# A down projection that runs one Winograd product at a time over all features, with act's operand sums stored by the up projection

## The chip, the cores and the metric

One Trainium2 chip, one core. The metric is the device time of one execution in microseconds (us). The kernel computes a whole decoder layer in one launch; the change lies in its last part, the feed-forward network.

## What is computed

The reference is one hybrid decoder layer over 2048 tokens of 1024 features in float32. The part that matters here is its feed-forward network:

```
def conv_gated_ffn(h, w_up, conv_w, conv_b, w_down):      # h: 2048 x 1024, w_up: 1024 x 8192, w_down: 4096 x 1024
    u = h @ w_up
    u_pad = jnp.pad(u, ((0, 0), (CONV_WIDTH - 1, 0), (0, 0)))
    u = conv_b + sum(conv_w[j] * u_pad[:, j:j + S] for j in range(CONV_WIDTH))
    gate, val = jnp.split(u, 2, axis=-1)
    return (jax.nn.gelu(gate, approximate=True) * val) @ w_down
...
        f = conv_gated_ffn(rms_norm(x, norm_ffn_pre[l]), w_ffn_up[l], conv_w[l], conv_b[l], w_ffn_down[l])
        x = x + rms_norm(f, norm_ffn_post[l])
```

## The kernel before

Phases a and b (normalisation, input projections, attention, the recurrent branch, the output projection) fill the first 1,215 us and are not touched. `phase_d` is the feed-forward network: the up projection, the convolution and the gate make `act` (4096 features by 2048 tokens), which goes to DRAM; the down projection reads it back and makes the output.

**Products in parts.** An operand is split into a high part (a cast on ScalarE, L40) and a low part (a subtraction on VectorE, L41), and a product of two blocks is three products of parts (`mm3`, L25 to L31). Every matmul of `phase_d` has a 128 x 128 stationary and a 128 x 512 moving operand.

**Up projection.** The work is 64 pairs n (32 pairs of a gate and a value block of 128 columns, for each half of 1,024 tokens). A pair is a 2 x 2 x 2 block product in Winograd's seven products j = 0 to 6, each 12 matmuls. `slots` is the order of the products; the pairs of two neighbours are interleaved, so that one product of another pair lies between two of one pair. `wprep` makes the weights' part `LEAD` = 6 products ahead. Each product has its own bank, and the eight banks go round; `post` combines them on VectorE: seven additions that read a bank for each pair (L284), and one copy on ScalarE (L289). Then the convolution (L275 to L277), GELU and the product with the value half follow, and 128 features by 1,024 tokens of `act` are stored (L308).

**Down projection.** Again Winograd's seven products, on blocks of 512 tokens (A) and 512 columns (B), for two halves h of the tokens and four groups g of 1,024 features: 56 steps (h, g, p) in the order `ORD` = P1, P5, P7, P6, P2, P3, P4 within each (h, g). A step is 4 blocks of 128 tokens, 12 matmuls each, 48 in all. `dload` loads a quarter of an operand (1 MB), `dprep` splits two of them (128 x 2048 each) one step ahead, and `dsums` makes Winograd's operand sums from the raw quarters, on GpSimd and VectorE (L191). Each block of a step goes into a bank and from there is copied (g = 0, L412) or added on VectorE (L414) to an accumulator in SBUF, one for each product. After the last group, `merge` (L395) adds the accumulators up, `square` (L378, L379) takes the sums of squares and scales by column, and `finish` (L386 to L391) norms, adds the residual and stores.

**Order.** The kernel's text gives dependencies and a priority; the framework orders each engine's instructions, and the DMA issues of each queue, when it builds the program. On the chip every queue then runs in that order. All DMAs of the part run on SyncE's queue, but for three at the start of the down projection.

Of the kernel before, what the change touches and what calls it, by code (L numbers as in the profile page):

```python
# [24 lines left out]
def mm3(nc, out, terms, first=True, last=True):  # L25
    """out += sum over terms of lhsT.T @ rhs, each operand an exact (hi, lo) pair"""
# [17 lines left out]
def rstd(nc, pool, ss, scale, eps, mhalf, tag):  # L44
    """(ss * scale + eps) ** -0.5"""
# [8 lines left out]
def bias_lines(nc, pool, psum, rel_bias, onehot, neg, line_d):  # L54
    """the bias of each relative position, masked, as 128 equal rows per head"""
# [12 lines left out]
def hsum(nc, pool, tag, h2t, hq, k):  # L68
    """Winograd's combinations of the blocks of h2 (features by tokens), for feature tiles k and k + 4"""
# [10 lines left out]
def conv_consts(nc, cw, pt, conv_w, conv_b, rows, ident):  # L80
    """the taps and the bias of the convolution, features on partitions: columns (tap, block)"""
# [8 lines left out]
LEAD = 6  # L90
# [3 lines left out]
def phase_d(ctx, tc, x1, h2t, w_up, cw, halo, w_down, g_post, mhalf, out, hq, act):  # L94
# [6 lines left out]
    with ExitStack() as es:  # L101
        rp = es.enter_context(tc.tile_pool(name="dr", bufs=2))
        # fourteen places of 8 KB
# [13 lines left out]
        def bank():  # L117
            """the eight banks in turn"""
            pss.append(pss.pop(0))
            return pss[-1].tile([P, 512], F32, tag="b", name="b")  # L120

        G = 8
        NG = NU // G
        NH = SEQ // SB
        ORD = ("P1", "P5", "P7", "P6", "P2", "P3", "P4")
        # operands of each product, in the places of the blocks that their sums replace
        OPS = {"P1": ("A11", "B11"), "P5": ("A21", "B11"), "P7": ("A11", "B12"), "P6": ("A11", "B11"),
               "P2": ("A12", "B21"), "P3": ("A12", "B22"), "P4": ("A22", "B21")}
        # sums made once a product is split: place, minuend, other, operation
        AFTER = {"P1": (("B11", "B12", "B11"), ("A11", "A11", "A21"), ("A21", "A22", "A21+"), ("B12", "B22", "B12")),  # L130
                 "P7": (("B11", "B22", "B11"), ("A11", "A22", "A11")),
                 "P2": (("A12", "A12", "A11"), ("B21", "B21", "B11"))}
        FREE = {"P5": ("A21",), "P7": ("B12",), "P2": ("A11", "B11"), "P3": ("A12", "B22"), "P4": ("A22", "B21")}
        wdv = w_down.rearrange("(j c p) d -> j p c d", p=P, c=G // 2)
# [3 lines left out]
        ACC = ({"P1": 10, "P5": 12, "P7": 2, "P6": 3, "P2": 13, "P3": 11}, {"P1": 10, "P5": 2, "P7": 3, "P6": 13, "P2": 11, "P3": 12})  # L138
        PARTS = ((4, 5, 6, 7), (0, 1, 8, 9))
        XT = {"A21": 8, "B12": 10, "A11": 12, "B11": 14}  # L140
        raw, dops, acc, pools, phases = {}, {}, {}, {}, []
        for h in range(NH):
            for g in range(NG):
                phases += [(h, g, p) for p in ORD]

        def dload(h, g, x, q=None):
# [6 lines left out]
            elif (h, g, x) == (0, 0, "B12"):  # L153
                t = big(ACC[0]["P3"], x, F32)
            else:
                t = pools["raw"].tile([P, 4, 512], F32, name=x)
# [1060 lines left out]
```

## Time and profile before

| | before |
|---|---|
| median of 3 runs (lowest to highest) | 3253.43 us (3253.23 to 3253.59) |
| span of the profiled execution, first to last instruction | 3251.4 us |
| TensorE busy | 3085.7 us, 95% of the span |
| VectorE busy | 2657.5 us, 82% |
| ScalarE busy | 1439.1 us, 44% |
| GpSimd busy | 1219.2 us, 37% |
| moved by DMA | 388.25 MB |

The profiled execution has no time of its own beside its span; the median of the runs is 2.0 us above that span, so the two agree to 0.1%. PE is TensorE's matmuls, PEld its weight loads, DVE VectorE, ACT ScalarE, POOL GpSimd, SP SyncE's queue. Matmuls are pipelined, so the durations of single matmuls overlap; the pace is read from how many fit into a stretch.

### The profile page before, as it was taken

How to read it: one execution, taken by the hardware profiler on the slowest of the kernel's cores; microseconds unless marked ns; L12 is line 12 of the kernel's file. 1: busy time of each engine (PE TensorE's matmuls, PEld its weight loads, DVE VectorE, ACT ScalarE, POOL GpSimd, SP SyncE). 2: the span in 40 equal slices, each digit the busy share in tenths (PEclk: the TensorE clock that was granted, in tenths of full speed). 3: DMA queues.
4: the chain of work that ended last, by engine and by line, in shares of the span. 5: the costliest groups of instructions: out<-in, count | busy, mean ns of one | idle time of the engine just before them, and what ended most of it. 6: DMA issues, size and time to landing. Idle time of an engine off the chain costs nothing. (4 is left out here: it accounts for less than half of the span.)

```text
span 3251.4 us, 46480 instructions
## 1 busy us (share of the span) xinstructions
PE 3085.7 (95%) x17897; PEld 2463.4 (76%) x17897; DVE 2657.5 (82%) x3535; ACT 1439.1 (44%) x2277; POOL 1219.2 (37%) x857
## 2 busy tenths in 40 slices
PE   5999999989999998899999999999999999889996
PEld 3888888777777777788888877888887777667775
DVE  4779786766767768999999999999998688886887
ACT  4565646354444454334444444444443533244322
POOL 1203122123334434533433433334333443784347
PEclk8999999979999999999999999999999999989998
DMA  5546463654445536422222342222223423142232
GB/s 134 143 137 180 131 169 105 186 170 119 133 120 174 180 122 206 144 84 85 85 78 78 97 150 78 79 90 85 78 78 105 154 104 104 65 155 104 104 104 78
DMA packets 476458, 388.25 MB, mean 119 GB/s; under 512 B 114042, under 2 KB 401100, under 8 KB 475212
## 3 DMA queue, kind: packets, MB, share of 16 engines
q1 hardware_dynamic: 474652, 382.13, 37.6%
q8 instruction: 141, 2.31, 0.3%
q10 hardware_dynamic: 1584, 3.15, 0.3%
q14 instruction: 81, 0.66, 0.1%
HBM read 276.68 MB, written 108.53 MB: 118 GB/s over the span
## 5 line engine op out<-in xcount | busy, mean ns | idle before, releaser
L30 PE MATMUL b<-hh,wh 128*128 128x512 f32 x1792 | 709.3, 396 | 18.5 <-DVE uv L284 12.8
L30 PE MATMUL b<-do 128*128 128x512 f32 x2688 | 651.4, 405 | 70.8 <-DVE do L41 54.7
L30 PE MATMUL b<-hl,wh 128*128 128x512 f32 x1792 | 710.2, 396 | 2.0 <-DVE hl L41 2.0
L30 PE MATMUL b<-hh,wl 128*128 128x512 f32 x1792 | 709.4, 396 | 0.4 <-DVE wl L41 0.4
L30 PEld LDWEIGHTS b<-do 128*128 128x128 f32 x2688 | 521.3, 195 | 200.7 <-DVE do L41 63.6
L40 ACT CAST wh<-wr 128x512 fp32r<-128x512 f32 (+1 forms) x400 | 279.8, 705 | 469.8 <-DMA wr<-in_w_ffn_up 152.7
L41 DVE TENSOR_TENSOR wl<-wr,wh 128x512 fp32r<-128x512 f32 (+1 forms) x400 | 368.6, 923 | 75.2 <-ACT wh L40 74.1
L30 PEld LDWEIGHTS b<-hh,wh 128*128 128x128 f32 x1792 | 338.2, 189 | 102.6 <-ACT wh L40 9.4
L30 PEld LDWEIGHTS b<-hl,wh 128*128 128x128 f32 x1792 | 338.3, 189 | 83.5 <-DVE hl L41 3.3
L30 PEld LDWEIGHTS b<-hh,wl 128*128 128x128 f32 x1792 | 338.3, 189 | 80.4 <-DVE wl L41 1.3
L237 POOL TENSOR_TENSOR s<-wr 128x512 f32<-128x512 f32 x64 | 133.6, 2087 | 610.2 <-DMA wr<-in_w_ffn_up 598.5
L30 PE MATMUL pj<-hh,wh 128*128 128x512 f32 x640 | 256.8, 402 | 27.8 <-ACT t L574 25.1
L30 PE MATMUL pj<-hh,wl 128*128 128x512 f32 x640 | 254.4, 398 | 0.1
L30 PE MATMUL pj<-hl,wh 128*128 128x512 f32 x640 | 254.1, 398 | 0.0
L41 DVE TENSOR_TENSOR do<-hr,do 128x2048 fp32r<-128x2048 f32 x48 | 151.1, 3151 | 47.2 <-ACT do L40 47.1
L40 ACT CAST do<-hr 128x2048 fp32r<-128x2048 f32 x48 | 90.5, 1905 | 212.9 <-PE b L30 131.3
L246 POOL TENSOR_TENSOR wr<-wr,s 128x512 f32<-128x512 f32 x64 | 140.4, 2193 | 110.8 <-DVE wl L41 110.7
L30 PEld LDWEIGHTS pj<-hh,wh 128*128 128x128 f32 x640 | 122.1, 191 | 56.1 <-ACT t L574 26.8
L414 DVE TENSOR_TENSOR acc<-acc,b 128x512 f32<-128x512 f32 x168 | 110.4, 679 | 44.8 <-PE b L30 44.8
L30 PEld LDWEIGHTS pj<-hh,wl 128*128 128x128 f32 x640 | 122.2, 191 | 27.2 <-DVE wl L41 0.9
L30 PEld LDWEIGHTS pj<-hl,wh 128*128 128x128 f32 x640 | 122.2, 191 | 25.9 <-DVE hl L41 0.2
L275 ACT ACTIVATE yg<-ug,cw 128x1024 f32<-128x1024 f32 x64 | 79.7, 1246 | 139.3 <-DVE ug L284 139.3
(290 smaller groups left out, 5847.8 us busy)
## 6 DMA issues: line engine op xcount, KB each, us to landing
wr<-in_w_ffn_up SPq DMA_DIRECT2D x128, 512.0 KB
wr<-in_w_in SPq DMA_DIRECT2D x64, 512.0 KB
d_act<-yg SPq DMA_DIRECT2D x64, 512.0 KB
B<-in_w_ffn_down SPq DMA_DIRECT2D x22, 1024.0 KB
wr<-d_act SPq DMA_DIRECT2D x16, 1024.0 KB
xt<-in_x SPq DMA_DIRECT2D x28, 512.0 KB
d_bk<-bk SPq DMA_DIRECT2D x16, 512.0 KB
wr<-in_w_in SPq DMA_DIRECT2D x32, 256.0 KB
```

The source lines that it names most:

```text
L30: nc.tensor.matmul(out=out, lhsT=a, rhs=b, start=first and i == 0 and j == 0, stop=last and i == n - 1 and j == 2)
L40: nc.scalar.copy(out=hi, in_=raw)
L41: nc.vector.tensor_tensor(out=lo, in0=raw, in1=hi, op=ALU.subtract)
L237: tt(out=r[1], in0=t[:, 2], in1=t[:, 3], op=ALU.add)
L246: tt(out=t[:, 1], in0=t[:, 1], in1=r[2], op=ALU.subtract)
L275: nc.scalar.activation(out=y, in_=u[:, 2:], func=AF.Identity, scale=w2c[:, col:col + 1], bias=bc[:, col:col + 1])
L414: nc.vector.tensor_tensor(out=o, in0=o, in1=pd, op=ALU.add)
```

## The change

**Up projection.** Products that are only added now add up in a bank: products 0, 2, 5 and 6 of a pair run into one bank (three banks take turns), product 1 into another, 3 and 4 into another (five take turns). Between two products of a bank its state is read: ScalarE copies it after products 0, 2, 3 and 6, VectorE adds it to something after 1, 4 and 5. That is three additions and four copies a pair, where there were seven and one. `LEAD` is 5 and there are 6 buffers of weight parts instead of 7. The second pair's products 1 to 6 no longer stand beside those of the first pair at the start.

**act.** Once two feature blocks are done, the seven operands that the down projection takes from them are stored, the four sums among them made on VectorE (2) and GpSimd (2): 1.75 MB for two pairs, where it was 1 MB.

**Down projection.** 56 steps (p, k): for each product p in the order P5, P3, P2, P1, P6, P7, P4 all eight groups k of 256 features (of each half of the features), for both halves of the tokens: 8 blocks of 6 matmuls in 8 banks. A bank is emptied only at the last k of a product, and P3, P6, P7 and P4 go on adding to what the product before them left in it. The sums of results that `merge` made are so made in the banks; P5, P3 and P2 end in a copy to SBUF, P1, P6 and P7 in an addition to it, P4 in the final norm straight from the bank. Each step loads its operand of act (1 MB) and one or two quarters of w_down's blocks (0.5 MB each); GpSimd makes the weights' sum for P5, P6, P7 and P4, and those of P5 and P6 are stored in DRAM (`td`) for P6 and P4.

The diff, cut to the lines that are added in `phase_d` (those that they replace are in the functions printed above):

```diff
...
+LEAD = 5
+WB = 6
...
+def phase_d(ctx, tc, x1, h2t, w_up, cw, halo, w_down, g_post, mhalf, out, hq, act, td):
...
         def places(st, ids, side):
...
         def big(i, name, dtype=F32R):
...
+        def bank(i):
+            return pss[i].tile([P, 512], F32, tag="b", name="b")
...
+        KC = 8
+        ORD = ("P5", "P3", "P2", "P1", "P6", "P7", "P4")
+        AIDX = {"P5": 0, "P6": 1, "P7": 2, "P3": 3, "P1": 4, "P2": 5, "P4": 6}
+        CHAIN = ("P3", "P6", "P7", "P4")
+        wdv = w_down.rearrange("(m c p) (d n) -> c d p m n", p=P, c=2, d=2)
...
+        phases = [(p, k) for p in ORD for k in range(KC)]
+        raw, dops = {}, {}
+        OPL = ((0, 1, 4), (5, 6, 7))
+        def dload(i):
...
+            p, k = phases[i]
+            ar = rp.tile([P, 2, 2, 512], F32, tag="hr", name="ar")
+            for h in range(NH):
+                nc.sync.dma_start(out=ar[:, h], in_=act[h][k][AIDX[p]].rearrange("m p t -> p m t"))
+            br = rp.tile([P, 2, 2, 512], F32, tag="wr", name="br")
+            w = lambda c, d: wdv[c, d, :, 2 * k:2 * k + 2, :]
+            t = lambda j: td[k][j].rearrange("m p n -> p m n")
+            src = {"P5": (w(0, 1), w(0, 0)), "P3": (w(1, 1),), "P2": (w(1, 0),), "P1": (w(0, 0),), "P6": (w(1, 1), t(0)),
+                   "P7": (w(1, 1), w(0, 1)), "P4": (w(1, 0), t(1))}[p]
+            for j, a in enumerate(src):
+                nc.sync.dma_start(out=br[:, j], in_=a)
+            if len(src) == 2:
+                nc.gpsimd.tensor_tensor(out=br[:, 0], in0=br[:, 0], in1=br[:, 1], op=ALU.subtract)
+            if p in ("P5", "P6"):
+                nc.sync.dma_start(out=t(p == "P6"), in_=br[:, 0])
+            raw[i] = ar, br
+        def dprep(i):
+            if i >= len(phases):
+                return
+            ar, br = raw.pop(i)
+            ah, al, b = (big(j, "do") for j in OPL[i % 2])
+            split(nc, b[:, 0:2], b[:, 2:4], br[:, 0])
+            split(nc, ah, al, ar.rearrange("p h k t -> p (h k) t"))
+            dops[i] = ah, al, b
...
+            wp = us.enter_context(tc.tile_pool(name="dw", bufs=WB))
...
             def hprep(half, j):
...
             def wprep(n, j):
...
+            banks, sums, us_, ys, even = {}, {}, {}, {}, {}
+            turn = [0]
             def product(n, j):
...
+                if j == 0:
+                    banks[n, "a"] = bank(n % 3)
+                elif j in (1, 3):
+                    banks[n, "b"] = bank(3 + turn[0] % 5)
+                    turn[0] += 1
+                o = banks[n, "b" if j in (1, 3, 4) else "a"]
+                for k in range(4):
+                    for i, (a, b) in enumerate(((wh, hh), (wh, hl), (wl, hh))):
+                        nc.tensor.matmul(out=o, lhsT=a[:, k, :], rhs=b[:, k, :], start=j in (0, 1, 3) and k == 0 and i == 0,
+                                         stop=k == 3 and i == 2, skip_group_check=True)
             def utile(n, b):
...
+                y = tp.tile([P, SB], F32, name="yg" if b == 0 else "yv", bufs=3 - 2 * b)
...
             def post(n, j):
...
+                a, b = banks.get((n, "a")), banks.get((n, "b"))
+                def add(out, x, y):
+                    nc.vector.tensor_tensor(out=out, in0=x, in1=y, op=ALU.add)
+                if j in (0, 2, 3):
+                    sums[n, j] = ep.tile([P, 512], F32, name="sum", bufs=3)
+                    nc.scalar.copy(out=sums[n, j], in_=b if j == 3 else a)
                 elif j == 1:
...
+                    add(utile(n, 0)[:, 2:514], sums.pop((n, 0)), b)
                 elif j == 4:
...
+                    add(us_[n, 0][:, 514:], sums.pop((n, 2)), b)
...
                 elif j == 5:
...
+                    add(utile(n, 1)[:, 514:], sums.pop((n, 3)), a)
...
+                    nc.scalar.copy(out=us_[n, 1][:, 2:514], in_=a)
...
+                    k, m = ff // 4, ff // 2 % 2
+                    dst = act[half][k][:, m].rearrange("j p t -> p j t")
+                    if ff % 2 == 0:
+                        nc.sync.dma_start(out=dst[:, 4], in_=y[:, :512])
+                        even[0] = y
+                        return
+                    nc.sync.dma_start(out=dst[:, 5:7], in_=y.rearrange("p (j t) -> p j t", j=2))
+                    e = even.pop(0)
+                    s = rp.tile([P, 4, 512], F32, tag="hr", name="sa")
+                    V, Q = nc.vector.tensor_tensor, nc.gpsimd.tensor_tensor
+                    Q(out=s[:, 2], in0=e[:, :512], in1=e[:, 512:], op=ALU.subtract)
+                    V(out=s[:, 0], in0=e[:, 512:], in1=y[:, 512:], op=ALU.add)
+                    V(out=s[:, 1], in0=s[:, 0], in1=e[:, :512], op=ALU.subtract)
+                    Q(out=s[:, 3], in0=y[:, :512], in1=s[:, 1], op=ALU.subtract)
+                    nc.sync.dma_start(out=dst[:, 0:4], in_=s)
...
+            pos = {14 * (n // 2) + 2 * j + n % 2 * 7: (n, j) for n in range(N) for j in range(7)}
+            pos[1] = pos.pop(7)
+            slots = [pos[k] for k in sorted(pos)]
...
                 if n == N - 1:
...
+                        dload(0)
+                    elif j == 3:
...
+                        dload(1)
...
+            xts, acc = {}, {}
+            APL = {"C22": (2, 3), "C12": (8, 9), "C11": (10, 11)}
+            def xload(t):
+                xts[t] = fp.tile([P, D], F32, name="xt", bufs=3)
+                nc.sync.dma_start(out=xts[t], in_=x1v[t])
+            def square(t, i, o):
+                junk = ep.tile([P, 512], F32, tag="sum", name="junk", bufs=3)
...
+            def scale(d, o):
+                nc.gpsimd.tensor_tensor(out=o, in0=o, in1=gpost[:, d * 512:d * 512 + 512], op=ALU.mult)
             def finish(t, parts):
...
+                    if o.space == PSUM:
+                        r = ep.tile([P, 512], F32, tag="sum", name="r", bufs=3)
+                        nc.vector.scalar_tensor_tensor(out=r, in0=o, scalar=rs, in1=gpost[:, ds], op0=ALU.mult, op1=ALU.mult)
+                        nc.vector.tensor_tensor(out=r, in0=r, in1=xt[:, ds], op=ALU.add)
+                        o = r
+                    else:
+                        nc.vector.scalar_tensor_tensor(out=o, in0=o, scalar=rs, in1=xt[:, ds], op0=ALU.mult, op1=ALU.add)
...
+            bks = {}
+            for i, (p, k) in enumerate(phases):
+                dprep(i + 1)
+                dload(i + 2)
+                ah, al, b = dops.pop(i)
+                last = k == KC - 1
+                if last and p in ("P6", "P4"):
+                    for q in range(3):
+                        xload(4 * (p == "P4") + q)
+                for h in range(NH):
+                    for q in range(4):
+                        n = h * 4 + q
+                        if k == 0 and p not in CHAIN:
+                            bks[n] = bank(n)
+                        for m in range(2):
+                            a = slice(q * P, q * P + P)
+                            for j, (x, y) in enumerate(((ah, m), (ah, 2 + m), (al, m))):
+                                nc.tensor.matmul(out=bks[n], lhsT=x[:, 2 * h + m, a], rhs=b[:, y], start=k == 0 and p not in CHAIN and m == 0 and j == 0,
+                                                 stop=last and m == 1 and j == 2, skip_group_check=True)
+                        if not last:
+                            continue
+                        t = h * 8 + q + 4 * (p in ("P7", "P4"))
+                        name = {"P5": "C22", "P3": "C12", "P2": "C11", "P1": "C11", "P6": "C12", "P7": "C22", "P4": "C21"}[p]
...
+                            square(t, 0, bks[n])
+                            finish(t, [bks[n], acc["C22", h][:, q]])
+                        else:
+                            if q == 0 and p in ("P5", "P3", "P2"):
+                                acc[name, h] = big(APL[name][h], "acc", F32)
+                            o = acc[name, h][:, q]
+                            if p in ("P5", "P3", "P2"):
+                                nc.scalar.copy(out=o, in_=bks[n])
+                            else:
+                                nc.vector.tensor_tensor(out=o, in0=o, in1=bks[n], op=ALU.add)
+                                square(t, p != "P1", o)
+                                scale(p != "P1", o)
+                            if p == "P6":
+                                finish(t, [acc["C11", h][:, q], o])
+                        if p in ("P6", "P4") and n < 5:
+                            xload((n + 3) // 4 * 8 + (n + 3) % 4 + 4 * (p == "P4"))
...
```

Outside `phase_d` only the DRAM tiles differ:

```diff
-    act = [dp.tile([8, P, SEQ], F32, name=f"d_act{j}") for j in range(4)]
+    act = [[dp.tile([7, 2, P, 512], F32, name=f"d_act{h}_{k}") for k in range(8)] for h in range(2)]
+    td = [dp.tile([2, 2, P, 512], F32, name=f"d_td{k}") for k in range(8)]
```

## Rows read from the trace of the kernel before

**Rows 1.** The page: busy us of each engine; 40 equal slices of the span, in tenths.

```profile
PE 3085.7 (95%) x17897; PEld 2463.4 (76%) x17897; DVE 2657.5 (82%) x3535; ACT 1439.1 (44%) x2277; POOL 1219.2 (37%) x857
...
PE   5999999989999998899999999999999999889996
...
PEclk8999999979999999999999999999999999989998
```

**Rows 2.** Windows: busy us (instructions) of PE, PEld, DVE, ACT, POOL; clock; DMA share; GB/s.

```profile
0.00:1215.00 1215.00, 1160.28 (x9753) 917.27 (x9755) 863.08 (x1754) 631.69 (x1307) 320.70 (x457) 0.97 0.51 147
1215.00:2511.00 1296.00, 1273.75 (x5464) 1024.86 (x5461) 1200.42 (x1424) 548.53 (x738) 508.04 (x281) 0.99 0.30 99
2511.00:3234.00 723.00, 651.62 (x2690) 521.29 (x2688) 580.47 (x339) 257.48 (x229) 381.17 (x108) 0.95 0.31 107
3234.00:3252.00 18.00, 0.00 (x0) 0.00 (x0) 13.55 (x21) 1.45 (x4) 9.32 (x14) 0.60 0.61 233
```

**Rows 3.** The same windows, a stretch inside the up projection.

```profile
1460.00:1622.00 162.00, 162.00 (x698) 130.96 (x697) 151.17 (x191) 66.16 (x93) 60.19 (x33) 1.00 0.27 85
```

**Rows 4.** Groups of PE, 1215 to 2511: busy, mean ns; idle before, releasers.

```profile
L30 PE MATMUL b<-hh,wh 128*128 128x512 f32 x1792 | 709.3, 396 | 18.5 <-DVE uv L284 12.8 <-ACT hTq L1107 3.5 <-DVE ug L284 1.2
```

**Rows 5.** Instructions by tile (do, acc): ns min/median/max, first and last start.

```profile
L40 ACT CAST do<-hr x48: 1890/1906/1917, 2497.3 to 3175.8; 128x2048 fp32r<-128x2048 f32 x48
L41 DVE TENSOR_TENSOR do<-hr,do x48: 2279/2293/6378, 2499.3 to 3177.8; 128x2048 fp32r<-128x2048 f32 x48
...
L414 DVE TENSOR_TENSOR acc<-acc,b x168: 672/676/690, 2609.6 to 3242.9; 128x512 f32<-128x512 f32 x168
L412 ACT COPY acc<-b x56: 564/587/593, 2521.1 to 2967.0; 128x512 f32<-128x512 f32 x56
...
L379 POOL TENSOR_TENSOR acc<-acc,gpost x16: 1288/1783/3350, 2850.1 to 3229.4; 128x512 f32<-128x512 f32 x16
```

**Rows 6.** Groups by form of the down projection, 2511 to 3252.

```profile
L30 PE MATMUL b<-do 128*128 128x512 f32 x2688 | 651.4, 405 | 70.8 <-DVE do L41 54.7 <-ACT do L40 16.0
...
L191 POOL TENSOR_TENSOR hr<-wr,hr 128x2048 f32<-128x2048 f32 x8 | 52.1, 6514 | 48.3 <-DVE do L41 48.3
...
L191 POOL TENSOR_TENSOR B<-B,hr 128x2048 f32<-128x2048 f32 x8 | 37.1, 4635 | 8.9 <-DVE do L41 8.9
...
L50 POOL TENSOR_TENSOR dnr<-dnv,mhalf 128x1 f32<-128x1 f32 x16 | 17.5, 1105 | 0.5
...
L48 POOL TENSOR_SCALAR dnv<-ssq 128x1 f32<-128x1 f32 x16 | 9.6, 597 | 1.3
L386 POOL TENSOR_TENSOR ssq<-ssq 128x1 f32<-128x1 f32 x16 | 7.6, 495 | 3.1 <-ACT junk L378 2.8
```

**Rows 7.** VectorE's timeline late in the up projection: start, us, instruction, idle before.

```profile
2474.93 1.27 DVE L277 SCALAR_TENSOR_TENSOR yg<-ug,cw,yg 128x1024 f32<-128x1024 f32 x1
2476.12 0.68 DVE L284 TENSOR_TENSOR sum<-sum,b 128x512 f32<-128x512 f32 x1
...
2478.51 0.68 DVE L284 TENSOR_TENSOR uv<-sum,b 128x512 f32<-128x512 f32 x1
...
2480.59 0.69 DVE L284 TENSOR_TENSOR uv<-sum,b 128x512 f32<-128x512 f32 x1 [0.21 <-PE b L30]
```

**Rows 8.** DMA in 40 slices each: 2511 to 2530; then 2511 to 3252.

```profile
GB/s 405 410 405 147 0 0 0 26 30 164 405 405 414 410 397 410 405 276 220 254 289 341 440 414 418 410 388 414 414 410 414 414 405 405 405 440 431 388 405 410
```

```profile
GB/s 329 131 1 236 105 41 73 68 274 0 114 1 225 116 1 114 1 170 171 13 157 305 75 292 9 62 53 165 176 1 113 44 245 52 57 57 48 67 1 226
```

**Rows 9.** TensorE's timeline where the first half of the tokens ends.

```profile
2888.24 4.17 PE L30 MATMUL b<-do 128*128 128x512 f32 x8 [9.32 <-ACT do L40]
2895.98 1.94 PE L30 MATMUL b<-do 128*128 128x512 f32 x4 [3.57 <-ACT do L40]
```

**Rows 10.** The timeline of the end: TensorE's last run, VectorE's last two instructions.

```profile
3210.35 23.05 PE L30 MATMUL b<-do 128*128 128x512 f32 x92 [4.67 <-DVE do L41]
```

```profile
3246.86 1.42 DVE L390 SCALAR_TENSOR_TENSOR acc<-acc,dnr,hr 128x512 f32<-128x512 f32 x2 [0.71 <-POOL dnr L50]
```

More of the change, by code (lines that the diff above doesn't have):

```diff
@@ L130, in phase_d @@
[L130 to L134, printed above, removed]
+        def bank(i):
+            return pss[i].tile([P, 512], F32, tag="b", name="b")
@@ L139, in phase_d @@
[L139 to L146, printed above, removed]
-            r, c = int(x[1]) - 1, int(x[2]) - 1
-            if x[1:] == "11":
-                t = rp.tile([P, 4, 512], F32, name="hr")
-            elif x[:2] == "A2":
-                t = rp.tile([P, 4, 512], F32, name="wr")
[L153 to L156, printed above, removed]
-            if x[0] == "A":
-                src = act[g].rearrange("(b c) p t -> b p c t", b=2)[c, :, :, h * SB + r * 512:h * SB + r * 512 + 512]
-            else:
-                src = wdv[g * 2 + r][:, :, c * 512:c * 512 + 512]
-            (q or nc.sync).dma_start(out=t, in_=src)
-            raw[x] = t
+        phases = [(p, k) for p in ORD for k in range(KC)]
@@ L252, in wprep @@
                 wops[n, j] = hi, lo
-            banks, sums, us_, ys = {}, {}, {}, {}
+            banks, sums, us_, ys, even = {}, {}, {}, {}, {}
+            turn = [0]
             def product(n, j):
                 (wh, wl), (hh, hl) = wops.pop((n, j)), hops[n // NU, j]
-                o = bank()
-                mm3(nc, o, [((wh[:, k, :], wl[:, k, :]), (hh[:, k, :], hl[:, k, :])) for k in range(4)])
-                banks[n, j] = o
+                if j == 0:
[8 more added lines that the diff above has]
+                                         stop=k == 3 and i == 2, skip_group_check=True)
             def utile(n, b):
@@ L307, in post @@
                     nc.vector.tensor_tensor(out=y, in0=y, in1=yv, op=ALU.mult)
-                    nc.sync.dma_start(out=act[ff // 8][ff % 8, :, half * SB:(half + 1) * SB], in_=y)
+                    k, m = ff // 4, ff // 2 % 2
[13 more added lines that the diff above has]
+                    nc.sync.dma_start(out=dst[:, 0:4], in_=s)
             N = 2 * NU
-            slots = [(n, j) for j in range(7) for n in range(2)]
-            pos = {14 * (n // 2) + 2 * j + n % 2 * 7: (n, j) for n in range(2, N) for j in range(7)}
-            slots += [pos[k] for k in sorted(pos)]
+            pos = {14 * (n // 2) + 2 * j + n % 2 * 7: (n, j) for n in range(N) for j in range(7)}
+            pos[1] = pos.pop(7)
+            slots = [pos[k] for k in sorted(pos)]
             wload(0)
@@ L389, in finish @@
                     ds = slice(i * 512, i * 512 + 512)
-                    nc.vector.scalar_tensor_tensor(out=o, in0=o, scalar=rs, in1=xt[:, ds], op0=ALU.mult, op1=ALU.add)
-                    nc.sync.dma_start(out=outv[t][:, ds], in_=o)
-            def merge(*pairs):
-                for eng, o, a in pairs:
-                    eng.tensor_tensor(out=acc[o], in0=acc[o], in1=acc[a], op=ALU.add)
-            V, Q = nc.vector, nc.gpsimd
-            MERGE = {"P1": ((Q, "P2", "P1"), (Q, "P6", "P1")), "P5": ((Q, "P3", "P5"),),
-                     "P6": ((V, "P3", "P6"), (V, "P7", "P6"), (Q, "P4", "P7"), (Q, "P5", "P7"))}
@@ L1176, in hybrid_layer @@
     phase_d(ctx, tc, x1, h2t, a["w_ffn_up"][0], cw, halo, a["w_ffn_down"][0], a["norm_ffn_post"],
-            mhalf, out[0], hq, act)
+            mhalf, out[0], hq, act, td)
 _VECS = ["w0", "a0", "k_k", "k_a", "r_k", "ln_x_g", "ln_x_b", "rwkv_shift_mix"]
```

104 lines of the change are left out of this document (removed).

## The prediction

> **What bounds the kernel now.** I read the page first: TensorE is busy for 95% of the span, and the slices show where it isn't: at the start, and in the last quarter, where the granted clock dips as well [rows 1]. The windows then cut the feed-forward part into its stages: the up projection from 1215 to 2511, the down projection from 2511 to about 3233, and a tail of 18 us without a matmul [rows 2]. A stretch inside the up projection gives the pace: 698 matmuls in 162.00 us with TensorE busy throughout and the clock at 1.00 (the 2.4 GHz level), so 0.2321 us each [rows 3]. That is the measure for both stages, since all their matmuls have one shape.
>
> The up projection has 5,376 of them: 5376 x 0.2321 = 1247.8 us. Another 88 in its window belong to phase b (13.7 us of busy time), so its floor is 1261.5 of the 1296 us. The remaining 34.5 us are 22.25 of idle time and some 12 of slower matmuls [rows 2]; 12.8 of the idle time is TensorE waiting for a bank that VectorE still reads [rows 4]. This stage is bound by TensorE already, with VectorE close behind: 151.17 of 162 us [rows 3]. The down projection has 2,688: 623.9 us at that pace, in 723. Of the 99 us between, 71 are idle, almost all in wait for a split operand [rows 6], and 28 are busy time above the pace, at a mean clock of 0.95 [rows 2]. So what the change can win is what the two stages spend above 1261.5 and 623.9, and a part of the tail; the number of matmuls stays the same.
>
> **The change, part by part.** *Steps of the down projection.* There are still 56, of 48 matmuls, 11.14 us each at full pace. Now VectorE has 580.47 us of work in the stage, 10.4 a step, nearly as much as TensorE [rows 2]. That is two splits of 2.29 us when alone and four additions of 0.68 [rows 5], its share of the sums, and time in which it stands behind GpSimd. After: one split of 128 x 2048 (2.29) and one of half that (1.15), 3.4 us a step; ScalarE has 1.91 + 0.95 = 2.9 [rows 5]. In the order cast, cast, subtraction the last part is ready some 5.5 us after the step before the last has freed its places, with 5.6 us to spare. GpSimd's weight sum is half a 128 x 2048 one, 2.3 us alone to 3.3 beside VectorE [rows 6], in four products of seven; it delays the split by as much at most and stays within the spare. So inside a product I expect no wait: cost 0, hidden behind 11.14 us of matmuls. Without that cover it would be 5.5 us a step.
>
> *Transfers.* A step loads 1.05 MB of act and 0.52 or 1.05 MB of weights, and P5 and P6 store 0.52 MB: 14.16 MB for each k, 113 MB in all, with x1 and the output 130 MB (198 GB/s over 656 us), where the stage moves 107 GB/s now [rows 2]. Pieces of 2 KB, as now, have run at 405 to 414 GB/s while nothing else was in the way, and at 329 over the first 18 us [rows 8]. A P5 or P6 step's 2.62 MB take 6.4 to 8.0 us of 11.14, and a load has about a step and a half from the time its buffer is free. I take 0; the other end, at a lower rate, is a rival below.
>
> *Ends of products.* P5, P3 and P2 end in eight copies of 0.59 us on ScalarE [rows 5], each with the seven other banks (9.7 us) before its bank is written again: 0. P1, P6 and P7 end in eight additions (0.68), squares, and eight scalings on GpSimd of 1.29 to 3.35 us [rows 5], and P6 also in eight finishes with three small GpSimd instructions each (0.50 + 0.60 + 1.11 = 2.2 us [rows 6]) and sixteen VectorE ones. At P6 GpSimd has 8 x 1.8 + 8 x 2.2 = 32 us of work, nearly three steps, and the weight sums for P7 and the splits stand in the same queues. The half's end now is the nearest row: TensorE waits there for 9.32 and 3.57 us [rows 9]. Bounds: 0 and three times those, 39; I take 12 for P6 and 4 each for P1 and P7, 20.
>
> *Change of stage.* P5's first block goes into bank 0, which still holds the last pair's last product; it waits for a copy of 0.59 us that may stand behind a cast of 1.91: 0.6 to 2.5, I take 2. Of the 28 us of slow matmuls now I leave 10, since the stalls come to about a third of the 71 us. Down projection: 623.9 + 20 + 2 + 10 = 656, which is 67 less than 723.
>
> *Up projection, work.* A pair takes 19.5 us of TensorE, 18.2 of VectorE, 8.0 of ScalarE, 7.2 of GpSimd (a 162 us stretch holds 698 / 84 = 8.31 pairs [rows 3]). Four additions of 0.68 go (-2.7), one sum of 128 x 512 for each pair comes (+0.7); VectorE 16.2. ScalarE gets three copies of 0.59: 9.8. GpSimd gets a sum of 1.3 (2.2 beside VectorE): 8.5 to 9.4. The added stores are 0.38 MB a pair on a stage at 99 GB/s [rows 2]. None reaches 19.5: cost 0 under the matmuls.
>
> *Up projection, waits.* New is that a product waits for a read of the bank that it goes on filling: product 4 for ScalarE's copy after 3, product 6 for VectorE's addition after 5. One product of the neighbouring pair lies between, 12 x 0.2321 = 2.79 us. How long does VectorE take now? The addition at 2480.59 started as its product ended (it had waited for PE), so products ended at 2480.4 and, two earlier, at 2474.8; that one is a product 5, and its two additions end at 2476.80 and 2479.19, 2.0 and 4.4 us later [rows 7]. What stands before them is a convolution step of 1.27. If the one addition that is left takes the place of the first, it is in time by 0.8 us; at the place of the second it is late by 1.6, or 102 us over 64 pairs. It is nearest to the first: it is now the first reader, and 2 us of other work a pair are gone. I take 8 in all. If ScalarE's copy stands behind one cast, it is there well within 2.79.
>
> The two sums on GpSimd speak against that place. A VectorE split of 2.29 us has taken up to 6.38 [rows 5], and GpSimd's 4.6 us sums 6.5 [rows 6]. The Trainium skill (SBUF — State Buffer, section Who interferes with whom) has it that a VectorE instruction with two SBUF inputs and a GpSimd one that reads SBUF exclude each other, the later waiting for the whole of the other. By that rule a 1.3 us sum before the addition would make every second pair late by about 0.5 us, 16 us instead of my 8.
>
> *Start of the up projection.* The 12.8 us of bank waits go in part, as VectorE has less to do; but the first pair's products 1 to 4 now follow each other at 2.79 us instead of 5.57, while an operand's cast and split take 1.9 and 2.3, one after the other, 4.2 us [rows 5]: 4 x 1.4 = 6 us lost. I take -8 in all. So the up projection comes out even: -8 + 8 = 0.
>
> *Tail.* TensorE ends at 3233.4, VectorE at 3248.3, the span at 3251.4 [rows 10]. After, each of the last eight blocks has three VectorE instructions of 0.7 (2.1 us) against 1.39 us of matmuls. 8 x 2.1 = 16.8, begun after 1.39 us of matmuls, a square of about a copy's 0.6 [rows 5] and GpSimd's 2.2 [rows 6], so 4.2 us into a step of 11.14, ends some 9.9 after it; with the same 3.1 us for the last store 13, which is 5 less than 18.
>
> Sum: 0 - 67 - 5 = -72 on a span of 3251.4; the runs' median is 2.0 above it, 3253.4 - 72 = **3181 us**.
>
> **Rivals.** *Reads in the bank hold up the up projection* (the one that ends on the other side). Place: product 6 behind VectorE, 64 times. The price of a late place is 1.6 us a pair, 3181 + 94 = 3275; it decides from 80 / 64 = 1.25 us a pair on, where nothing is left. For it: the second addition's 4.4 us. Against it: that the first comes after 2.0, and VectorE's room. Chance 0.15, about half of it slower.
>
> *Transfers pace the down projection.* The means of whole stages lie between 99 and 233 GB/s [rows 2]; if no more than 200 could be held, P5's and P6's 2.62 MB would take 13.1 us a step, 16 x 2.0 = 32 more: 3213. For it: loads, sum and store of a step stand in one queue. Against: 405 GB/s bursts, and slices with next to no traffic [rows 8], so the present rate is no limit. Chance 0.13.
>
> *The ends of products cost the full 39 us, and the clock with them*: +19 and +6, 3206. For it: rows 9. Chance 0.12.
>
> *The splits stay late anyway*, because the queues' order doesn't fit and TensorE waits as now: only the tail's 5 and nothing else, 3248. Chance 0.05.
>
> **How the numbers follow.** My forecast has 0.55: 3181, between 3135 (no late reads, no ends, most of the start's loss gone: -46) and 3215. The range reaches down to 3125 and up over the second, third and fourth rival and the milder half of the first, to 3250; what it leaves out is the harsher half of the first (0.07), and something below 3125, for which the floors leave room (1261.5 + 623.9 would be 3115): about 0.15 in all. Within 0.2% (6.5 us) of 3253.4 is about what a measurement of this kernel can tell from no change. Faster 0.55 + 0.13 + 0.12 + half of the first rival, 0.87, of which I take 0.02 off for what I don't see: 0.85. Same is the fourth rival, 0.05; slower the other half of the first and that rest, 0.10.
>
> **What would show it.** Right: in the down projection about 650 us from first to last matmul, clock above 0.97, idle time only at ends of products and most at P6's; waits for `do` gone; GpSimd's scalings the longest thing beside; DMA near 200 GB/s with no empty slices. In the up projection about 1296 us, TensorE's waits split between the start and ACT's and VectorE's reads. Wrong: idle TensorE before product 6 or 4 of each pair (waits for uv L284 or a sum's copy), loads that end the waits of casts in P5 and P6, or a down projection with stalls in every step.

## The result and the profile after

The median is 3166.0 us (3165.56 to 3166.63, 4 runs) against 3253.51 for the kernel before on the same chip (4 runs): ratio 0.9727 [0.9713, 0.9741], 87.5 us less. The forecast was 3181, with 3125 to 3250 as its range. The profiled execution's span is 3164.5 us, 86.9 less than before's.

The page of the kernel after, in the parts of [rows 1]:

```profile
PE 3057.7 (97%) x17897; PEld 2450.0 (77%) x17897; DVE 2321.7 (73%) x3171; ACT 1460.4 (46%) x2437; POOL 1104.2 (35%) x903
...
PEclk8999999979999999999999999999999999999999
```

Its windows by stage, then the stretch of [rows 3] and two of the down projection:

```profile
0.00:1215.00 1215.00, 1160.26 (x9766) 916.76 (x9766) 863.72 (x1753) 632.00 (x1308) 321.91 (x459) 0.97 0.51 147
1215.00:2512.00 1297.00, 1267.97 (x5418) 1021.57 (x5419) 1173.34 (x1233) 632.91 (x928) 619.16 (x340) 0.99 0.36 117
2512.00:3148.00 636.00, 629.44 (x2715) 511.67 (x2713) 275.62 (x174) 192.90 (x197) 158.06 (x93) 0.99 0.56 195
3148.00:3165.00 17.00, 0.00 (x0) 0.00 (x0) 9.00 (x14) 2.63 (x8) 5.07 (x12) 0.55 0.75 288
1460.00:1622.00 162.00, 162.00 (x699) 131.15 (x699) 146.53 (x167) 78.97 (x116) 74.15 (x42) 1.00 0.33 106
2512.00:2592.00 80.00, 77.76 (x336) 62.46 (x335) 45.23 (x27) 24.33 (x20) 25.86 (x9) 1.00 0.78 286
2860.00:2950.00 90.00, 90.00 (x393) 73.36 (x392) 36.06 (x25) 27.90 (x32) 33.21 (x16) 1.00 0.72 245
```

The groups of TensorE, of the up projection's bank waits and of the down projection:

```profile
L243 PE MATMUL b<-hh,wh 128*128 128x512 f32 x1792 | 705.3, 397 | 20.5 <-DVE uv L269 17.1
...
L392 PE MATMUL b<-do 128*128 128x512 f32 x2688 | 623.5, 394 | 5.2 <-DVE do L41 4.0
```

What to see: the stretch of [rows 3] holds 699 matmuls where it held 698, without a gap. The down projection's 2,688 matmuls take 623.5 us (the floor was 623.9) and 5.2 idle us, where it was 651.4 and 70.8 [rows 6]. The window from 2512 also holds 27 matmuls of the up projection, because TensorE's order, made anew when the program is built, mixes the last pair with the first step. With one wait of 1.0 us they take some 7 us, which I count with the up projection. By stages, forecast and measured: up projection 1296 and 1297 + 7 = 1304; down projection 656 and 623.5 + 5.2 = 629; tail 13 and 17 (the last matmul ends at 3147.7, the span at 3164.5). So +8, -27 and +4: 15 us less than forecast.

### The profile page after: what moved, and what is told of

It reads as the page before. It is cut to its first block, busy times and chain, and to the rows that moved or that the text cites. A ratio compares the mean times of both kernels' runs of the same rounds, so it can differ in the third digit from the quotient of the medians.

```text
span 3164.5 us, 46753 instructions
## 1 busy us (share of the span) xinstructions
PE 3057.7 (97%) x17897; PEld 2450.0 (77%) x17897; DVE 2321.7 (73%) x3171; ACT 1460.4 (46%) x2437; POOL 1104.2 (35%) x903
## 3 DMA queue, kind: packets, MB, share of 16 engines
q8 instruction: 140, 2.29, 0.3%
## 4 chain that ended last, share of the span: by engine, by line
PE 81%; DVE 8%; DMA 4%; issue 2%; ACT 2%; POOL 1%; SPq 1%; DVEq 0%; POOLq 0%; ACTq 0%
PE b L243 32%; PE b L392 17%; PE pj L30 13%; PE m L30 5%; PE pp L869 2%; DVE wl L41 2%; DMA wr<-in_w_ffn_up 1%; PE po L1036 1%; PE lo L570 1%; PE pt L1028 1%; PE sc L1004 1%; PE px L893 1%; PE pgt L949 1%; PE pu L903 1%; PE psn L910 1%
## 5 line engine op out<-in xcount | busy, mean ns | idle before, releaser
L243 PE MATMUL b<-hh,wh 128*128 128x512 f32 x1792 | 705.3, 397 | 20.5 <-DVE uv L269 17.1
L392 PE MATMUL b<-do 128*128 128x512 f32 x2688 | 623.5, 394 | 5.2 <-DVE do L41 4.0
L392 PEld LDWEIGHTS b<-do 128*128 128x128 f32 x2688 | 507.2, 189 | 121.1 <-DVE do L41 4.8
L41 DVE TENSOR_TENSOR wl<-wr,wh 128x512 fp32r<-128x512 f32 (+1 forms) x400 | 448.1, 1121 | 93.9 <-ACT wh L40 90.8
L41 DVE TENSOR_TENSOR do<-ar,do 128x2048 fp32r<-128x2048 f32 x56 | 135.1, 2412 | 314.4 <-ACT do L40 314.4
L212 POOL TENSOR_TENSOR s<-wr 128x512 f32<-128x512 f32 x64 | 126.2, 1971 | 481.5 <-DMA wr<-in_w_ffn_up 372.6
L40 ACT CAST do<-ar 128x2048 fp32r<-128x2048 f32 x56 | 106.8, 1907 | 371.8 <-PE b L392 359.0
L153 POOL TENSOR_TENSOR br<-br 128x1024 f32<-128x1024 f32 x32 | 95.9, 2998 | 461.1 <-DMA br<-d_td 361.1
L279 ACT ACTIVATE yg<-yg 128x1024 f32<-128x1024 f32 x64 | 68.0, 1062 | 223.5 <-DVE yg L261 223.5
L213 POOL TENSOR_TENSOR s<-s,wr 128x512 f32<-128x512 f32 x64 | 134.1, 2095 | 5.4 <-DVE wl L41 0.6
```

Of the source, the lines that this page charges most:

```text
L40: nc.scalar.copy(out=hi, in_=raw)
L41: nc.vector.tensor_tensor(out=lo, in0=raw, in1=hi, op=ALU.subtract)
L153: nc.gpsimd.tensor_tensor(out=br[:, 0], in0=br[:, 0], in1=br[:, 1], op=ALU.subtract)
L212: tt(out=r[1], in0=t[:, 2], in1=t[:, 3], op=ALU.add)
L213: tt(out=r[2], in0=r[1], in1=t[:, 0], op=ALU.subtract)
L243: nc.tensor.matmul(out=o, lhsT=a[:, k, :], rhs=b[:, k, :], start=j in (0, 1, 3) and k == 0 and i == 0, stop=k == 3 and i == 2, skip_group_ ...
```

## Experiments

In all of them times are medians where there were several runs; differences are to the 3166.0 of the kernel after, unless the text says otherwise. They ran on three chips, where the kernel before took 3252.65 to 3254.04 us. The kernels with one run have no interval; where there are several runs, those of one kernel lie 1 to 8 us apart, so a difference of a few us means something only where the trace shows it too.

**1. What made the old down projection wait?** My prediction named VectorE's load. The rivals are the emptying of the banks by itself, and the chain of operand sums, each of which waits for raw operands and holds up a split. Three kernels put load of the old kind on the new one, and two take a part from the old one. A GpSimd sum of 128 x 2048 in each of 54 steps:

```diff
+            if i >= 2:
+                w = ar.rearrange("p h k t -> p (h k) t")
+                nc.gpsimd.tensor_tensor(out=big(12, "x", F32), in0=w, in1=w, op=ALU.add)
```

> Against the changed kernel (3166 us). Added: in every step from the third on one GpSimd sum of 128 x 2048 over the step's loaded act operand (4.6 us alone), as the kernel before made in six of seven steps; its result is not used. Theory: VectorE's split of 2.3 us stands behind it for at most 4.6 us, the operand is ready 10 us into a step of 11.14, so 0 to 20 more. Rival: GpSimd's sums alone made the splits late: 50 to 100 more.

Measured: 3178.41, +12 (the added sum takes 3.60 us alone, not the 4.6 of the old ones). Eight reads of a bank on VectorE in each step but the last of a product, 392 in all:

```diff
+                            d = ep.tile([P, 512], F32, tag="sum", name="dr", bufs=3)
+                            nc.vector.tensor_tensor(out=d, in0=gpost[:, :512], in1=bks[n], op=ALU.add)
```

> Against the changed kernel (3166 us; down projection 636 us). Added: in every step of the down projection but the last of a product, eight VectorE additions of 128 x 512 that read the eight banks, as the kernel before had to do to empty them; their result is not used. That is 5.4 us a step on VectorE, 10.2 in all, against TensorE's 11.14. Theory: the old stage's waits came from VectorE's load together with its standing behind GpSimd's sums; the bank reads alone still fit: 0 to 15 more. Rival: reading the banks out each step was the cause by itself: 50 to 100 more.

Measured: 3177.37, +11. Both together:

> Against the changed kernel (3166 us). Both additions at once: eight bank reads on VectorE and a GpSimd sum of 128 x 2048 in every step. Theory: VectorE's 10.2 us and up to 4.6 us in which it stands behind GpSimd come to 14.8, over TensorE's 11.14: 60 to 150 more, with TensorE waiting for the splits (do L41) as before the change. Rival: neither matters and it was the order of the products that freed the splits: less than 30 more.

Measured: 3189.73, +24, the sum of the two. The window of its down projection:

```profile
2512.00:3170.00 658.00, 636.12 (x2706) 513.44 (x2706) 597.23 (x564) 193.12 (x194) 382.53 (x146) 0.98 0.54 187
```

VectorE has 597 us and GpSimd 383 here, as much as the old stage had (580 and 381 [rows 2]), and the stage takes 658, not 723. Almost all of TensorE's 20.9 us of waits stand at the start and behind P6's end; in between, 40 steps run without one:

```profile
2536.88 446.19 PE L395 MATMUL b<-do 128*128 128x512 f32 x1921 [6.06 <-DVE dr L399]
```

So a load of this size, spread over the steps, does not by itself make TensorE wait in them; it costs about a quarter of what the change won. That it costs the same in the old order is not shown. On the old kernel, the other way: leaving out the additions of its results in two of its four groups (112 of 168),

```diff
-                    else:
+                    elif g == NG - 1:
```

> The kernel before (3253 us), with 112 of the 168 additions left out that empty a bank of the down projection (groups 1 and 2 of each half; the output lacks those partial sums and is not the reference's). Theory (the chain of sums): these additions take 76 us of VectorE's time but end no chain, so at most 10 to 15 us less: 3238 to 3253. Rival (VectorE's load of 10.4 us a step): 40 us less or more, 3213 or below.

Measured: 3250.19, 3 below the 3253.5 of the kernel before, which is less than its own runs differ by, and TensorE still waits at the beginnings of the groups, 4.4 to 4.5 us once in 336 matmuls (67.2 us in all, where it was 70.8):

```profile
2982.58 80.44 PE L30 MATMUL b<-do 128*128 128x512 f32 x336 [4.52 <-DVE do L41]
3067.41 79.22 PE L30 MATMUL b<-do 128*128 128x512 f32 x336 [4.38 <-DVE do L41]
3151.09 22.86 PE L30 MATMUL b<-do 128*128 128x512 f32 x88 [4.46 <-DVE do L41]
```

And leaving out its operand sums (the splits take the raw quarters instead):

```diff
-            if i and p in AFTER:
-                dsums(p)
...
-                        dsums("P1", 0, 3)
...
-            dsums("P1", 3)
```

> The kernel before (3253 us, its down projection 723 us), with one thing left out: the operand sums of the down projection on GpSimd and VectorE (L191), so that the products are made of the plain quarters and the output is not the reference's. The load experiments have shown that neither VectorE's bank reads nor GpSimd's sums cost more than 12 us as mere load. New theory: it is their place in a chain: at the start of each group of seven steps a split waits for a sum, that sum for another on GpSimd, and that for the split of the step before; TensorE waits 5 to 9 us there, eight times, and its clock falls. Without the sums 40 to 70 us go: 3183 to 3213; what is left over the new kernel are the waits at the ends of the halves. Rival: the waits belong to the ends of the halves and to VectorE's load: 3240 or more.

Measured: 3168.27, 85 less than before and as fast as the change itself. Its down projection, and all the idle time of TensorE in it, five waits where there were 22:

```profile
2511.00:3150.00 639.00, 623.70 (x2680) 506.44 (x2678) 428.08 (x316) 251.90 (x226) 117.70 (x63) 0.99 0.34 118
```

```profile
PE b L30 <- DVE do L41: 12.2, 5, 2.7
```

The kernel before shows where the waits stood and how a sum makes one. In two of its groups, of 336 matmuls each, TensorE does 329 without a wait:

```profile
2618.59 78.10 PE L30 MATMUL b<-do 128*128 128x512 f32 x329 [4.52 <-DVE do L41]
2703.79 77.81 PE L30 MATMUL b<-do 128*128 128x512 f32 x329 [3.09 <-DVE do L41]
```

Of its 70.8 idle us, 52 stand in the first two steps of the eight groups; without the sums 2.7 are left there. The other 19 stand in the last group of each half, where the merges run too; 9.4 are left. The 28 us of slow matmuls are gone as well (623.7 us busy, 651.6 before), at a granted clock of 0.99 instead of 0.95. The timelines of GpSimd, VectorE, ScalarE and TensorE at one beginning of a group:

```profile
2678.50 4.61 POOL L191 TENSOR_TENSOR hr<-hr,wr 128x2048 f32<-128x2048 f32 x1 [21.52 <-DVE do L41]
2683.18 6.53 POOL L191 TENSOR_TENSOR wr<-wr 128x2048 f32<-128x2048 f32 x1
```

```profile
2678.88 6.38 DVE L41 TENSOR_TENSOR do<-hr,do 128x2048 fp32r<-128x2048 f32 x1
...
2685.78 6.09 DVE L191 TENSOR_TENSOR hr<-B,hr 128x2048 f32<-128x2048 f32 x1
...
2693.92 4.82 DVE L41 TENSOR_TENSOR do<-hr,do 128x2048 fp32r<-128x2048 f32 x1 [0.86 <-ACT do L40]
```

```profile
2691.98 1.91 ACT L40 CAST do<-hr 128x2048 fp32r<-128x2048 f32 x1 [14.14 <-DVE hr L191]
```

```profile
2698.79 1.91 PE L30 MATMUL b<-do 128*128 128x512 f32 x7 [2.11 <-DVE do L41]
```

Read it in order of time: GpSimd's first sum is in place and waits for a split of the quarter (until 2678.4); VectorE's next split and its own sum each stand beside a GpSimd sum and take 6.4 and 6.1 us instead of 2.3; the cast has waited 14.1 us for that sum; its split ends at 2698.7 and TensorE starts. Nothing of this appears in a busy share; it is a chain of five instructions on three engines, once for each group of seven steps. The experiment takes out the chain and the sums' load together; e8_both puts such a load at 24 of the 85, in the new order.

**2. Does adding up in a bank make room for act's sums?** Each product back in its own bank, with seven additions and one copy, the rest as after; its core:

```diff
-                o = banks[n, "b" if j in (1, 3, 4) else "a"]
+                o = banks[n, j] = bank(turn[0] % 8)
+                turn[0] += 1
...
-                    sums[n, j] = ep.tile([P, 512], F32, name="sum", bufs=3)
-                    nc.scalar.copy(out=sums[n, j], in_=b if j == 3 else a)
...
+                elif j == 2:
+                    add(sums[n], sums[n], o)
```

> Against the changed kernel (3166 us). Undone: the products of the up projection that add up in a bank; each product has a bank of its own again, with seven additions on VectorE and one copy on ScalarE a pair, all else as in the changed kernel, act's sums too. Theory: VectorE has 17.6 us a pair now, with four additions of 0.68 more 20.3, more than TensorE's 19.5, so it becomes the bound: 0.8 x 64 = 51 us more, 3217 (3200 to 3240). Rival: VectorE has the room and the up projection stays TensorE's: 3166 within 8, or less, as the reads in the bank are gone.

Measured: 3235.29, +69. The stretch of [rows 3] in it, and TensorE's bank waits from 1215 to 2512:

```profile
1460.00:1622.00 162.00, 153.57 (x655) 122.12 (x654) 147.28 (x191) 60.56 (x88) 62.94 (x38) 1.00 0.30 98
```

```profile
PE b L239 <- DVE uv L265: 62.6, 53, 5.0
```

655 matmuls instead of 699, and 53 waits behind VectorE. It works 18.9 us a pair (147.28 over 655 / 84 pairs), not the 20.3 that I expected, and stands 1.9 more behind ScalarE; together 20.8, over TensorE's 19.5, so its queue is the bound. 69 of the 87 us that the change won would be gone. The same sums left out of the kernel after (four raw blocks stored in their place, the same bytes):

```diff
-                    Q(out=s[:, 2], in0=e[:, :512], in1=e[:, 512:], op=ALU.subtract)
-                    V(out=s[:, 0], in0=e[:, 512:], in1=y[:, 512:], op=ALU.add)
...
+                    for z, t in enumerate((e, y)):
+                        nc.sync.dma_start(out=dst[:, 2 * z:2 * z + 2], in_=t.rearrange("p (j t) -> p j t", j=2))
```

> Against the changed kernel (3166 us). Left out: the four operand sums of act in the up projection (two on VectorE, two on GpSimd for two pairs); the same 1 MB is stored from the unsummed tiles, so the output is not the reference's. Theory: in the steady stretch the sums cost nothing, since TensorE is busy throughout with them (699 matmuls in 162 us); only near the start and the change of halves, where product 6 waits 16 us in all for VectorE's addition, some of it comes back: 3158 to 3166. Rival: the sums on GpSimd hold VectorE up all along: 3150 or less.

Measured: 3156.64, -9.7. With the banks' help the sums cost some 10 us (one run), not 0, and none of it in the steady stretch, which has 698 matmuls here and 699 with them; from 1785 to 2110 there are 1366 here and 1322 with them.

**3. The order that leaves no product between.** The prices of late reads rest on one product of the neighbour between two of a pair. Here the order says there is none:

```diff
-            pos = {14 * (n // 2) + 2 * j + n % 2 * 7: (n, j) for n in range(N) for j in range(7)}
-            pos[1] = pos.pop(7)
-            slots = [pos[k] for k in sorted(pos)]
+            slots = [(n, j) for n in range(N) for j in range(7)]
```

> Against the changed kernel (3166 us). One edit: the products of a pair stand one after the other in the text's order, without another pair's product between them. Theory: the interleaving hides the reads in the bank; without it product 4 waits for ScalarE's copy after 3 and product 6 for VectorE's addition after 5, about 1 to 2 us each with what stands before them in the queues: 64 x 2 x 1 to 2 = 130 to 250 us more, 3296 to 3416. Rival: the read is short enough (0.6 to 0.7 us) and the framework puts other products between them on its own: less than 40 us more.

Measured: 3159.39, -7. My expectation fell. The order written down is a priority, and the stretch of [rows 3] holds 699 matmuls without a gap here too; products of one pair in a row, each waiting for a copy of 0.58 us, could not do that, so the framework must have mixed the products of neighbours by itself. So this run says nothing on the price of a missing product between; it shows only that in this order half of the bank waits (7.9 of 15.4 us) are for ScalarE's copies.

**4. The change of halves.** In the up projection's second half the operand of tokens is split in pieces of 128 x 2048, which keep VectorE for 2.3 us at a time. In four pieces:

```diff
-                n = HPIECE if half == 0 else 4
+                n = HPIECE if half == 0 else 1
```

> Against the changed kernel (3166 us). One edit: the operands of the second half of the tokens are split in four pieces of 128 x 512 instead of one of 128 x 2048. Theory: at the change of halves (1785 to 2110, 17 us lost) product 6 waits for VectorE's addition, which stands behind such a split of 2.3 to 2.8 us; in pieces of 0.68 the addition comes in between and 5 to 8 us come back: 3158 to 3161. Rival: the operands themselves are late (loads, casts), and nothing changes: 3166 within 2, or some us more for the extra instructions.

Measured: 3158.4 (3153.59 to 3159.68), ratio 0.9707 [0.9694, 0.972], -7.6. From 1785 to 2110 there are 1349 matmuls instead of 1322, and the waits for VectorE's bank reads are 2.8 us instead of 7.0. The time came as expected, but the way is not shown: those waits end at 1936, 1956 and 1979, and the last split of tokens had ended at 1909, so the late additions do not stand directly behind one. The stretch:

```profile
1785.00:2110.00 325.00, 316.94 (x1349) 253.57 (x1348) 299.87 (x329) 164.60 (x252) 149.80 (x80) 0.99 0.37 120
```

**5. The tail.** ScalarE's timeline at the end of the kernel after: the squares wait for stores, since their target `junk` and the stored `r` take turns in the same three buffers.

```profile
3151.93 0.60 ACT L354 ACTIVATE junk<-b 128x512 f32<-128x512 f32 x1 [3.37 <-DMA out<-r]
...
3154.46 0.60 ACT L354 ACTIVATE junk<-b 128x512 f32<-128x512 f32 x1 [1.84 <-DMA out<-r]
```

Buffers of its own for `r`:

```diff
-                        r = ep.tile([P, 512], F32, tag="sum", name="r", bufs=3)
+                        r = fp.tile([P, 512], F32, name="r", bufs=4)
```

> Against the changed kernel (3166 us, tail 17.2 us from TensorE's end to the end of the span). One edit: the buffer r of the last step gets four buffers of its own instead of sharing three with the squares' scratch. Theory: in the last step ScalarE's squares wait until the stores of r have read the shared buffers (rows of 1.84 to 3.37 us), and VectorE waits for what follows from them; apart, VectorE's 8 x 2.1 us set the tail and it is 13 us, so 3162, 4 less. Rival: VectorE's three instructions for each block set it already, and nothing changes (3166 within 1).

Measured: 3165.69 (3163.31 to 3167.76), ratio 0.9732 [0.9719, 0.9745], no difference. The squares' waits are gone, but the end of the span is 16.0 us behind the last matmul (3145.6) instead of 16.8 (the 17.2 in the expectation takes that matmul's end 0.4 us too early): VectorE now waits for rows of x1, whose buffers come free as late.

```profile
3156.86 0.69 DVE L369 TENSOR_TENSOR r<-r,xt 128x512 f32<-128x512 f32 x1 [1.84 <-DMA xt<-d_x]
```

**6. Together.** The edits of 4 and 5, and eight buffers for the rows of x1, loaded ahead:

```diff
-                xts[t] = fp.tile([P, D], F32, name="xt", bufs=3)
+                xts[t] = fp.tile([P, D], F32, name="xt", bufs=8)
...
-                    for q in range(3):
-                        xload(4 * (p == "P4") + q)
+                    for q in range(8):
+                        xload(q // 4 * 8 + q % 4 + 4 * (p == "P4"))
```

> The changed kernel (3166 us) with three edits: four buffers of its own for r in the last step; x1's rows for all eight blocks loaded at the start of the last step of P6 and of P4, in eight buffers instead of three; the second half's operands split in pieces of 128 x 512. The run with r's own buffers showed the next wait in line, VectorE waiting for x1's rows whose buffers were not free, and its tail was 16 us. Theory: with those rows there early VectorE sets the tail, 13 us (-4), and the pieces bring 7 as before: 3155 (3151 to 3158). Rival: the early rows get in the way of the steps' operands on SyncE's queue: 3158 or more, with waits for do at P6's end.

Measured: 3159.0 (3155.3 to 3160.83), ratio 0.9706 [0.9693, 0.9719], no better than the change of halves alone. The tail is down to 11.5 us (3147.2 to 3158.7). But in the order that the framework makes with the rows loaded early, VectorE does the last eight of P6's finishing instructions in one run of 7.5 us, the split for P7 stands behind it, and TensorE waits 8.4 us, where it was 3.2 with the change of halves alone:

```profile
2980.27 7.48 DVE L372 SCALAR_TENSOR_TENSOR acc<-acc,dnr,xt 128x512 f32<-128x512 f32 x8 [1.83 <-POOL dnr L50]
```

```profile
2991.14 156.04 PE L392 MATMUL b<-do 128*128 128x512 f32 x664 [8.42 <-DVE do L41]
```

The same with the order of experiment 3:

> The kernel with those three edits, and the up projection's products in the plain order of the text (pair after pair), which the framework interleaves on its own; alone that gave 3159.4 in one run. Theory: the gains lie in different places (start and change of halves by order, change of halves by pieces, tail), so some of them add up: 3146 to 3154. Rival: order and pieces remove the same waits at the change of halves: the same as with the three edits, within 3 us.

Measured: 3161.68 (3160.61 to 3163.12), ratio 0.9718 [0.9705, 0.9731]. The gains of the two do not add up: in the plain order TensorE waits 11.4 us for ScalarE's copies and 6.0 for VectorE's reads in the up projection, and 8.0 at P6's end.

## Why the prediction was right, by its steps

**Direction and place: right.** The down projection lost its waits for splits and goes at TensorE's pace, the steady up projection is unchanged. The price of the step, 11.14 us of matmuls over 6.3 of casts and splits, held: the casts of act's operands now stand idle for 359 us behind TensorE, which waits for none of them but one (1.25 us).

**The reason in it: incomplete.** I read 10.4 us of VectorE work a step against 11.1 of TensorE as what made the splits late. Experiment 1 shows that the same load in the new order costs 24 us, its waits at the start and behind P6's end. What went with the old operand sums is 85 us, 49 of it idle time at the beginnings of the groups; so some 60 us were the sums' place in the chain, if the load is worth the same in the old order. A count of the waits behind [rows 6] would have shown it: the 70.8 us are 22 waits of up to 9.3 us, too few for 56 steps that are each too full.

**Ends of products and clock: 32 us taken, 5 measured.** This is the term that was mis-sized most. I took [rows 9] as the nearest, but those waits went with the old sums: without them 2.7 us are left at that place. Only P6's end costs more than 2 us:

```profile
2554.16 431.82 PE L392 MATMUL b<-do 128*128 128x512 f32 x1873 [1.25 <-ACT do L40]
2989.97 157.70 PE L392 MATMUL b<-do 128*128 128x512 f32 x671 [3.99 <-DVE do L41]
```

P1's and P7's eight additions and squares hide, as P5's copies do. P6's place was right (the finishes wait for GpSimd, and the split stands behind), at 4 us and not 12. With no stalls there are no slow matmuls either: the 10 us for the clock are 0, as 623.5 of 623.9 shows. The third rival falls with them, and so does the fourth.

**Transfers: right.** 195 GB/s over the stage (198 forecast), 286 in P5's steps and 245 in P6's, at a TensorE busy for 97 and 100%. The second rival falls.

**Up projection: 0 taken, +8 measured.** VectorE has 17.6 us of work a pair (146.53 over 699 / 84 pairs), not 16.2, still under TensorE's 19.5. Count its matmuls by stretch. From 1460 to 1785 and from 2110 to 2500 before and after have as many, and no wait for a read of a bank: the 8 us for those reads were 0. Up to 1460 it is 902 against 894, so 2 us were gained at the start and not 8. The loss is at the change of halves, which I had not priced. The kernel before and the one after, from 1785 to 2110:

```profile
1785.00:2110.00 325.00, 319.98 (x1364) 256.85 (x1363) 307.94 (x361) 143.26 (x186) 122.56 (x65) 0.99 0.31 101
```

```profile
1785.00:2110.00 325.00, 311.60 (x1322) 250.14 (x1321) 291.45 (x302) 161.30 (x230) 151.04 (x78) 0.98 0.36 119
```

42 matmuls fewer are 9.7 us; without act's sums there are 1366, with smaller splits 1349. So 0 - 2 + 10 = 8. The first rival's mechanism exists, but only after the start and after the change of halves, not in the steady stretches: the 17.1 us behind VectorE's reads are 8 waits, 9.1 us from 1300 to 1460, 7.0 from 1785 to 2110, and the one of 1.0 at the end. The last splits of tokens end at 1271 and 1909, before these waits; what makes VectorE's additions late there stays open.

**Tail: 13 taken, 16.8 measured.** The sum of VectorE's work was right and the buffers were not counted: the squares shared three with the stores' source. Removing that alone showed the next wait of the same kind (experiment 5).

The terms' errors, +8, -27 and +4, leave the time 15 us below the forecast. That it came so near is in part luck: the errors have both signs, and in the up projection a loss of 10 us that I had not priced stands against one of 8 for late reads that did not come. Not settled: how the 60 us split between the waiting for raw quarters and the slowed instructions of the chain.

## What to carry to other kernels

A stage in which the helping engine is busy for 80% can still be a chain problem: count the waits before you divide busy time by steps, and follow one of them back through the queues. Move a sum that stands between a load and a split to the place where its operands are made, if that place has room, and make the room first; here accumulating in the banks was worth 69 us to the sums. A buffer tag shared by two tiles couples engines that have nothing else to do with each other, and taking such a wait away can bring up the next one.

## Unexpected on the hardware

VectorE's subtraction of two SBUF operands and a GpSimd sum don't share time, they take turns, to 0.15 us. GpSimd and VectorE in the kernel with a sum in each step:

```profile
2704.05 3.60 POOL L168 TENSOR_TENSOR x<-ar 128x2048 f32<-128x2048 f32 x1 [7.79 <-DMA ar<-d_act]
...
2726.75 5.37 POOL L168 TENSOR_TENSOR x<-ar 128x2048 f32<-128x2048 f32 x1 [7.68 <-DMA ar<-d_act]
```

```profile
2704.25 5.55 DVE L41 TENSOR_TENSOR do<-ar,do 128x2048 fp32r<-128x2048 f32 x1 [4.70 <-ACT do L40]
...
2726.37 2.29 DVE L41 TENSOR_TENSOR do<-ar,do 128x2048 fp32r<-128x2048 f32 x1 [4.01 <-ACT do L40]
```

The first sum ends at 2707.65; 2.29 later is 2709.94, and the subtraction that began beside it ends at 2709.80. The other way round, the subtraction ends at 2728.66, 3.60 later is 2732.26, and the sum ends at 2732.12. This is what the Trainium skill says (SBUF — State Buffer, section Who interferes with whom), and here the traces agree with it to 0.15 us. What I had not expected is how little it costs when the work has slack: one more sum in each of 54 steps costs 12 us, at VectorE's splits of 3.7 us instead of 2.4 in the mean. In the up projection the 8 us that I took for late reads, 16 by that rule, were 0 in the steady stretches; the 192 additions from a bank took 0.67 to 0.69 us each, beside GpSimd's sums or not.
